# A recorded order of issue that counts the port VectorE and GpSimd share, and prices dense matmuls at 2.25 columns a ns

## Chip, cores and metric

The kernel runs on one core of one Trainium2 chip. The metric is the device time of one launch in microseconds (us): 2947.76 us before, the median of three runs (2943.65 to 2950.33). Engines are named as the profile names them: PE is TensorE (PEld its weight loads), DVE is VectorE, ACT is ScalarE, POOL is GpSimd, and SP is the queue from which nearly all DMAs are issued.

## What is computed

One layer of a hybrid encoder, 2048 prompt frames and 32 sample frames wide, 1024 features, float32 in and out. Cut to what matters here:

```python
def layer(x, ...):
    hn = rmsnorm(x, norm1)
    proj = jnp.einsum('btd,de->bte', hn, w_in)             # 1024 -> 3072
    pa_x, pa_g = proj[..., :D_A], proj[..., D_A:2 * D_A]   # RG-LRU, 256 wide
    pb = proj[..., 2 * D_A:2 * D_A + D_B_IN]               # RWKV-7, 6 heads of 64
    pc = proj[..., 2 * D_A + D_B_IN:]                      # mLSTM, 6 heads of 64
    ...
    ya = rmsnorm(h, norm_a) * jax.nn.gelu(pa_g)
    yb, shift_new, S_new = rwkv7_mix(pb, ...)              # a state carried from frame to frame
    yc, conv_c_new, C_new, n_new, m_new = mlstm_mix(pc, ...)
    y_mix = jnp.concatenate([ya, yb, yc], axis=-1)
    x = x + jnp.einsum('bte,ed->btd', y_mix, w_out)
    hn2 = rmsnorm(x, norm2)
    gu = jnp.einsum('btd,df->btf', hn2, w_ffn_in)          # 1024 -> 2 * 2816
    x = x + jnp.einsum('btf,fd->btd', jax.nn.silu(gu[..., :D_FF]) * gu[..., D_FF:], w_ffn_out)
```

The layer's outputs are the normed x and the running states of the three mixers.

## The kernel before

**Dense work.** Features lie on the partitions, frames on the columns. The 2080 frames are four column blocks: three of 512 and one of 544, which is worked as two halves of 272. Every projection is done in three matmuls for one, because weights and activations are split into a leading part and an exact rest: with `wh`, `wl` the weight's parts and `ah`, `al` the activation's, `mm3` issues `wh*ah`, `wh*al` and `wl*ah` into one PSUM tile `pj`. So the stages are, in dense matmuls: `inproj` 24 tiles x 8 row tiles x 3 = 576 a block, 1152 for the last one with its two halves, 2880 in all; `phase2` (output projection, FFN) 64 x 3 + 44 x 8 x 3 + 8 x 22 x 3 = 1776 a block, and 3552 for the last. Together 11760. Weights come by DMA (`raw`); ACT writes their leading part (`wh`, `hh`), DVE or POOL the rest (`wl`, `hl`).

**Mixers.** Between them stand the mixers: 16 groups of 128 prompt frames (0 to 15) and one of the 32 sample frames (group 16), each an RWKV-7 part (tiles `rw`), an mLSTM part (`ml`) and an RG-LRU part. A group's RWKV part is one chain through all engines: low-rank gates, key norms, the products `m1<-Fr,BK`, a round trip through DRAM (`tb<-Hr`, `xs<-tb`), a triangular solve of 31 steps on DVE (`utmp<-Z,xs`, then `Z<-Z,utmp`), a second round trip (`zb<-Z`, `c<-zb`), DVE's transpose `ta<-c`, the state's products on PE, a head norm on DVE (`hmE` to `yx`), three transposes on PE (`rw<-cst,yx`), and the result `E` to DRAM (`ymix<-E`). Groups follow each other through the state `S` and share their tiles.

**Which stage needs which group.** `phase2(i)` reads `ymix` of four groups, `sq<-ymix` and the split `al<-sq,ah`; `phase2(3)` that of groups 12 to 16. Row tiles 0 and 1 of `ymix` are RG-LRU's, 2 to 4 RWKV's, 5 to 7 mLSTM's, and a PSUM tile takes them in this order.

**Order of issue.** Nothing is issued when the code is run: a `Recorder` notes each instruction with its operands (`Recorder.add`) and gives it a price from `cost`. `Recorder.order` then plays the program through: the engine that can start first takes its most urgent instruction that is ready, and the sequence in which they were taken is the order in which each engine's queue is filled. Engines then run their queues strictly in that order. On PE the mixers (level 1) stand before the projections (level 2), but in bursts: their prices add to a `debt`, and the projections pay it back,

```python
                elif o.prio == 2:
                    debt -= o.dur * RATE
```

with `RATE` 0.45. So a price that is too low or too high moves nothing by itself: it decides how many dense matmuls stand between two steps of a mixer. Before the change a dense matmul of n columns was priced n / 2.4 + 2.7 ns (216.0 for 512, 116.0 for 272), and DVE and POOL ran side by side in the plan without any hold on each other.

Of the kernel before, what the change touches and what calls it, by code (L numbers as in the profile page):

```python
# [27 lines left out]
# columns of the per-feature vectors, 128 features a column  # L28
# [13 lines left out]
# columns of the constants  # L42
# [11 lines left out]
# columns of the small weights  # L54
# [41 lines left out]
class Cfg:  # L96
    def __init__(self, seq, sb1, sb2):
        # sb1: list of (prompt tokens, column blocks); the 32 sample tokens follow the last prompt token
        # sb2: list of (first column, column blocks)
        self.seq = seq  # L100
        self.T = seq + 32
        self.sb1 = sb1
        self.sb2 = sb2
# [10 lines left out]
# PE's share for the mixers, relative to the projections, and how long they may hold it at a time (ns)  # L114
RATE = 0.45
BURST = 1200.0
# allowance for the mixers' operands (ns)
# [13 lines left out]
# transfers issued ahead of the one under way (ns)  # L131
WINDOW = 3000.0
# the projection's tile before which the next columns are normed
NEXT = 14
# urgency, on the other engines and on PE; the lowest goes first
# [8 lines left out]
class Op:  # L144
    __slots__ = ("eng", "fn", "args", "kw", "dur", "lat", "prio", "succ", "need", "ready", "start", "end", "idx", "rank")


class Recorder:
    """Stands in for the engines: notes each instruction with its operands, so that the order of issue
    can be chosen before the instructions are emitted (under tc.manual_schedule, which keeps it)."""  # L150
# [49 lines left out]
    def add(self, eng, fn, name, args, kw):  # L200
# [12 lines left out]
        o.dur, o.lat = cost(eng, name, out, ins, kw)  # L213
        deps = set()
# [29 lines left out]
    def order(self):  # L244
        """greedy: the engine that can start first takes its most urgent instruction that is ready"""
# [5 lines left out]
        debt, burst = 0.0, False  # L251
        for o in self.ops:
            o.rank = (o.prio, o.idx)
            if o.need == 0:
                heapq.heappush(future[o.eng], (0.0, o.rank, o))
        out = []
        left = len(self.ops)
        while left:
# [36 lines left out]
            if best == "pe":  # L295
# [3 lines left out]
                elif o.prio == 2:  # L299
# [3 lines left out]
                    burst = False  # L303
            o.start = when
# [43 lines left out]
def cost(eng, name, out, ins, kw):  # L348
    """nanoseconds on the engine, and until another engine sees the result"""
# [8 lines left out]
    if eng == "pe":  # L358
# [3 lines left out]
        if st.dtype == F32R:  # L362
            return max(n, 256) / 2.4 + 2.7, 196.0
# [25 lines left out]

class Tiles:  # L390
    """fixed tiles, taken in turn: name -> bufs tiles"""
# [30 lines left out]
def hybrid_kernel(ctx, tc, A, O, cfg):  # L422
# [48 lines left out]
    def rsqrt_(x, y, t, it=3):  # L471
        """y = 1/sqrt(x), Newton from the exponent halved"""
# [7 lines left out]
    def log1p_(e, out2, tmp):  # L480
        """out2 = log(1+e)/2 for 0 <= e <= 1, by the series of atanh(e/(2+e)); tmp: two tiles"""
# [10 lines left out]
    # the gates' weights, row selections; histories and running states: stream 0 the prompt, 1 the sample  # L492
# [11 lines left out]
    def setup():  # L504
# [9 lines left out]
        # derived vectors  # L514
# [8 lines left out]
        # -4 softplus(-lam)  # L523
# [8 lines left out]
        # powers of two of silu's halves and of the key's scale  # L532
# [4 lines left out]
        # the gates' weights for the queries and keys, from the heads' input: wq wif_q + wk wif_k  # L537
# [18 lines left out]
        # wq wk^T: queries for keys that are the heads' input itself  # L556
# [5 lines left out]
        # selection rows for row terms in two parts  # L562
# [4 lines left out]
        # histories and running states  # L567
# [23 lines left out]
    def load_w(src, kt, eng=None, many=False, into=None):  # L591
        """a block of weights, split: (hi, lo) of each row tile. Two small ones share a slot;
        many: the hidden units' tiles serve as two slots more; into: tiles that are free"""
# [1044 lines left out]
```

## Time and profile before

| | before |
|---|---|
| three runs | 2943.65, 2947.76, 2950.33 us |
| profiled execution, span from first to last instruction | 2943.6 us, as the fastest of the three runs |
| PE busy | 2797.9 us (95%), granted clock 0.979 of full speed |
| DVE busy | 2190.3 us (74%) |
| ACT busy | 1217.7 us (41%) |
| POOL busy | 704.9 us (24%) |
| DMA | 317.95 MB, mean 108 GB/s |

A busy PE is not a PE at its peak: its matmuls are pipelined, and an instruction's duration (some 360 ns for a dense one) is longer than the time to the next. What a dense matmul takes is therefore read from long unbroken rows of them, and what PE loses from its idle time.

### The profile page before, as it was taken

The numbers are of one execution on the slowest core, as the hardware profiler recorded it, in microseconds if no ns is written. First come the engines' busy times: TensorE is split into PE (matmuls) and PEld (weight loads), VectorE is DVE, ScalarE is ACT, GpSimd is POOL, SyncE is SP. The second block draws the span as 40 slices with busy tenths as digits, with TensorE's granted clock in tenths as the row PEclk, the third lists the DMA queues.
The fourth block names the chain that finished last, engine by engine and source line by source line (L and its number), as shares of the span: only waits on it lengthen the run. The fifth ranks groups of instructions, "written<-read, shape, count | busy, mean of one in ns | idle before, by whom it ended". The sixth has DMA issues, their size and how long they took to land.

```text
span 2943.6 us, 48657 instructions
## 1 busy us (share of the span) xinstructions
PE 2797.9 (95%) x17643; PEld 2301.3 (78%) x17643; DVE 2190.3 (74%) x5580; ACT 1217.7 (41%) x2555; POOL 704.9 (24%) x839
## 2 busy tenths in 40 slices
PE   7989889989999999999999999999999999999998
PEld 6767667778877777777777777777777778999998
DVE  6776887777778877888888887888666776555555
ACT  4444454444454434445544444363433334322223
POOL 5644344344312011112311011122011112211102
PEclk9999999999999999999999999999999999999999
DMA  6353334253433233324433323334332334232222
GB/s 210 112 160 109 123 123 128 100 165 100 122 100 98 82 104 99 91 72 128 139 111 92 96 87 101 93 107 138 93 107 82 93 87 162 74 90 87 87 90 81
DMA packets 235212, 317.95 MB, mean 108 GB/s; under 512 B 63100, under 2 KB 146988, under 8 KB 234844
## 3 DMA queue, kind: packets, MB, share of 16 engines
q1 hardware_dynamic: 233820, 313.74, 35.0%
q8 instruction: 138, 2.26, 0.3%
q10 hardware_dynamic: 1152, 1.11, 0.1%
q14 instruction: 102, 0.84, 0.1%
HBM read 268.51 MB, written 46.27 MB: 107 GB/s over the span
## 4 chain that ended last, share of the span: by engine, by line
PE 61%; DVE 20%; DMA 5%; issue 2%; ACT 2%; POOL 1%; SPq 0%; DVEq 0%; ACTq 0%; POOLq 0%
PE pj L332 51%; PE rw L332 7%; DVE wl L332 4%; PE ml L332 3%; DMA xs<-tb 3%; DVE utmp L332 1%; DVE Z L332 1%; DVE stg L332 1%; DVE x L332 1%; DVE k L332 1%; DMA tb<-Hr 1%; DVE Fr L332 1%; DVE R L332 1%; DVE al L332 1%; DVE Dm L332 1%
## 5 line engine op out<-in xcount | busy, mean ns | idle before, releaser
L332 PE MATMUL pj<-ah,wh 128*128 128x512 f32 (+1 forms) x2560 | 905.8, 361 | 4.1 <-ACT cbuf L332 1.8
L332 PE MATMUL pj<-al,wh 128*128 128x512 f32 (+1 forms) x2560 | 903.8, 360 | 4.4 <-DVE al L332 4.4
L332 PE MATMUL pj<-ah,wl 128*128 128x512 f32 (+1 forms) x2560 | 836.4, 358 | 2.0 <-DVE wl L332 2.0
L332 ACT ACTIVATE wh<-raw 128x1024 fp32r<-128x1024 f32 (+2 forms) x444 | 382.2, 862 | 759.2 <-PE pj L332 587.5
L332 PEld LDWEIGHTS pj<-ah,wh 128*128 128x128 f32 x2560 | 488.6, 191 | 73.1 <-issue 2.7
L332 PEld LDWEIGHTS pj<-al,wh 128*128 128x128 f32 x2560 | 490.7, 192 | 69.2 <-DVE al L332 6.0
L332 PEld LDWEIGHTS pj<-ah,wl 128*128 128x128 f32 x2560 | 458.8, 191 | 71.4 <-DVE wl L332 3.0
L332 DVE TENSOR_TENSOR wl<-raw,wh 128x1024 fp32r<-128x1024 f32 (+2 forms) x397 | 412.6, 1041 | 61.7 <-ACT wh L332 58.7
L332 POOL TENSOR_TENSOR stg<-stg,rb 128x512 f32<-128x512 f32 (+1 forms) x110 | 155.2, 1419 | 893.8 <-DVE stg L332 771.0
L332 PE MATMUL pj<-hl,wh 128*128 128x512 f32 (+1 forms) x856 | 302.2, 360 | 2.7 <-DVE hl L332 2.1
L332 PE MATMUL pj<-hh,wh 128*128 128x512 f32 (+1 forms) x856 | 299.7, 361 | 3.5 <-ACT hh L332 3.5
L332 PE MATMUL pj<-hh,wl 128*128 128x512 f32 (+1 forms) x856 | 279.5, 356 | 0.0
L332 DVE TENSOR_TENSOR x<-x,pj 128x512 f32<-128x512 f32 (+1 forms) x280 | 159.1, 583 | 134.9 <-PE pj L332 133.2
L332 PEld LDWEIGHTS pj<-hl,wh 128*128 128x128 f32 x856 | 161.6, 189 | 28.3 <-DVE hl L332 7.0
L332 PEld LDWEIGHTS pj<-hh,wh 128*128 128x128 f32 x856 | 160.1, 188 | 28.8 <-ACT hh L332 6.7
L332 PE MATMUL pj<-ah,hh 128*128 128x512 f32 (+1 forms) x480 | 173.1, 367 | 7.3 <-ACT hh L332 5.8
L332 PE MATMUL pj<-al,hh 128*128 128x512 f32 (+1 forms) x480 | 174.7, 370 | 2.5 <-DVE al L332 2.5
L332 DVE TENSOR_TENSOR utmp<-Z,xs 96x60 f32<-96x60 f32 (+27 forms) x527 | 135.7, 258 | 51.1 <-DMA xs<-tb 36.4
L332 PEld LDWEIGHTS pj<-hh,wl 128*128 128x128 f32 x856 | 152.3, 188 | 22.3
L332 POOL TENSOR_TENSOR wl<-raw,wh 128x1024 fp32r<-128x1024 f32 x47 | 114.8, 2444 | 191.1 <-ACT wh L332 186.9
L332 PE MATMUL pj<-ah,hl 128*128 128x512 f32 (+1 forms) x480 | 160.1, 365 | 0.0
L332 POOL TENSOR_TENSOR hl<-raw,hh 128x512 fp32r<-128x512 f32 x92 | 126.7, 1379 | 114.6 <-ACT hh L332 106.1
(348 smaller groups left out, 4222.1 us busy)
## 6 DMA issues: line engine op xcount, KB each, us to landing
raw<-in_w_ffn_in SPq DMA_DIRECT2D x176, 512.0 KB
raw<-in_w_ffn_out SPq DMA_DIRECT2D x128, 256.0 KB
raw<-in_w_in SPq DMA_DIRECT2D x96, 256.0 KB
raw<-in_w_in SPq DMA_DIRECT2D x48, 512.0 KB
spill<-stg SPq DMA_DIRECT2D x72, 256.0 KB
raw<-in_w_out SPq DMA_DIRECT2D x32, 512.0 KB
x<-in_xT SPq DMA_DIRECT2D x48, 256.0 KB
raw<-in_w_ffn_out SPq DMA_DIRECT2D x64, 192.0 KB
```

Of the source, the lines that this page charges most:

```text
L332: o.fn(*o.args, **o.kw)
```

## The change

Two things are changed, and both only in the numbers by which the order is worked out. No instruction is added, removed or altered: each engine has the same work as before, in another order.

- A dense matmul of n columns is priced max(n, 256) / 2.25 + 4 ns: 231.6 for 512 columns, 124.9 for 272.
- An instruction is marked by `shares` when it is POOL's and has an input, or DVE's and has two inputs in SBUF that are wider than a column, or is a copy or a tensor-scalar with one such input. In the plan a marked one of DVE starts only when POOL's last marked one has ended, and the other way round.

The rest of the diff takes comments out.

```diff
@@ class Recorder, add
         o.dur, o.lat = cost(eng, name, out, ins, kw)
+        o.port = shares(eng, name, ins)
@@ order
         debt, burst = 0.0, False
+        port = {"dve": 0.0, "pool": 0.0}
...
                     burst = False
+            if o.port:
+                other = "pool" if best == "dve" else "dve"
+                when = max(when, port[other])
+                port[best] = when + o.dur
             o.start = when
@@ cost
         if st.dtype == F32R:
-            return max(n, 256) / 2.4 + 2.7, 196.0
+            return max(n, 256) / 2.25 + 4.0, 196.0
@@
+def shares(eng, name, ins):
+
+    wide = [a for a in ins if a.space != PSUM and not (len(a.ap) == 2 and int(a.ap[1][1]) == 1)]
+    if eng == "pool":
+        return bool(ins)
+    if eng == "dve":
+        return len(wide) > 1 or (len(wide) == 1 and len(ins) == 1 and name in ("tensor_copy", "tensor_scalar"))
+    return False
```

The two orders differ on every engine from the first rows on. Two places of PE's queue follow. The first is where group 3 ends, the last group that `phase2(0)` reads. In the order of before this is the row at which the last three transposes of group 3 stand (`rw_165<-cst_75,yx_169`), among dense matmuls of `inproj(3)` (`pj` from `ah`, `al` and the weight tiles `wh`, `wl`, 272 columns):

```order
L332 MATMUL pj_199<-ah_0_174,wh_143 128x272
L332 MATMUL pj_199<-al_0_175,wh_143 128x272
L332 MATMUL pj_200<-ah_0_174,wh_143 128x272
L332 MATMUL pj_200<-al_0_175,wh_143 128x272
L332 MATMUL pj_199<-ah_0_174,wl_145 128x272
L332 MATMUL pj_200<-ah_0_174,wl_145 128x272
L332 MATMUL rw_165<-cst_75,yx_169 128x128 x3
L332 MATMUL rw_166<-cl_123,bones_81 128x384
```

2274 dense matmuls stand ahead of these transposes, 606 fewer than `inproj` has. In the order of the change the same group is here only at the products that follow its solve (`rw_166<-ta_167,Hr_125`, the transposed block times `Hr`), and `inproj` is used up; the dense matmuls of 512 columns are the first of `phase2(0)`, from row tile 1:

```order
L338 MATMUL pj_198<-ah_0_172,wh_143 128x512
L338 MATMUL pj_198<-al_0_173,wh_143 128x512
L338 MATMUL pj_198<-ah_0_172,wl_145 128x512
L338 MATMUL ml_164<-cst_75,f_0_269 6x128
L338 MATMUL ml_164<-q_262,xi_261 64x64 x3
L338 MATMUL ml_163<-RS_84,selr_83 128x130 x3
L338 MATMUL rw_166<-ta_167,Hr_125 32x32 x12
L338 MATMUL ml_163<-cst_75,xi_261 128x128 x2
L338 MATMUL rw_165<-c_168,En_226 32x32 x12
L338 MATMUL rw_166<-SV_150,Fr_124 64x64 x6
L338 MATMUL ml_163<-cst_75,xi_261 128x128
L338 MATMUL rw_165<-zc_229,c_168 64x64 x6
```

What moved: 12 matmuls of `phase2(0)` stand ahead, those of row tiles 0 and 1; the next dense one, from `ah_0_174` (row tile 2, RWKV's), comes 46 rows after these 12 dense ones, and all rows between are mixers'. Group 3's last transposes stand behind 2892 dense matmuls.

The second place is group 16, the last that `phase2(3)` reads. In the order of before its chain has dense matmuls of `phase2(2)` (512 columns) between its steps; 212 of them stand between the first `rw` row here and the chain's row before it:

```order
L332 MATMUL pj_201<-ah_0_170,wh_142 128x512
L332 MATMUL pj_201<-al_0_171,wh_142 128x512
L332 MATMUL rw_165<-ta_167,Hr_125 32x32 x6
L332 MATMUL pj_201<-ah_0_170,wl_144 128x512
L332 MATMUL pj_201<-ah_0_172,wh_142 128x512
L332 MATMUL pj_201<-al_0_173,wh_142 128x512
L332 MATMUL pj_201<-ah_0_172,wl_144 128x512
L332 MATMUL rw_166<-c_168,En_226 32x32 x6
L332 MATMUL rw_165<-SV_150,Fr_124 64x64 x4
L332 MATMUL pj_201<-ah_0_174,wh_142 128x512
```

In the order of the change `phase2(2)` is used up. The dense rows are the last that `phase2(3)` has without RWKV's tiles (272 columns, row tile 1), and behind them stands the chain of group 16 from its key norms on: `zc`, the bonus `ch`, `cl`, the transposes `yx`, `m1` (`Fr_124,BK_240`), the block's transposes, the state:

```order
L338 MATMUL pj_200<-al_0_173,wh_143 128x272
L338 MATMUL pj_200<-ah_0_172,wl_145 128x272
L338 MATMUL rw_166<-cst_75,zc_229 64x96
L338 MATMUL rw_166<-ch_122,bones_81 128x192
L338 MATMUL rw_166<-cl_123,bones_81 128x192
L338 MATMUL rw_165<-cst_75,yx_169 128x64 x3
L338 MATMUL rw_165<-Fr_124,BK_240 128x128 x3
L338 MATMUL rw_166<-Fr_124,BK_240 128x128 x3
L338 MATMUL rw_165<-cst_75,BK_240 128x128 x3
L338 MATMUL rw_166<-cst_75,xs_223 64x128 x3
L338 MATMUL rw_165<-SV_150,Fr_124 64x64 x2
L338 MATMUL rw_165<-ta_167,Hr_125 32x32 x6
```

What moved: all of this chain, down to its last three transposes 13 rows further on, stands in PE's queue without a dense matmul between. Counted over the whole order, the dense matmuls ahead of a group's last transposes, beside the number at which the stage that reads it begins, are:

| last group read | stage begins after | before | change |
|---|---|---|---|
| 3, by `phase2(0)` | 2880 | 2274 | 2892 |
| 7, by `phase2(1)` | 4656 | 4261 | 4668 |
| 11, by `phase2(2)` | 6432 | 6063 | 6444 |
| 16, by `phase2(3)` | 8208 | 8166 | 8232 |

At groups 7 and 11 the rows between the last dense matmul and the first from row tile 2 begin later in the chain than at group 3: at 7 with the last products of the outputs (`rw<-SV,Fr`, `rw<-Un,Hr`), at 11 with the same products a few rows earlier, and 45 and 66 matmuls stand there, the mixers' but for eight at each.

## Rows read from the trace of the kernel before

**Rows 1.** The profile's page: span, busy time by engine, chain that ended last.

```profile
span 2943.6 us, 48657 instructions
PE 2797.9 (95%) x17643; PEld 2301.3 (78%) x17643; DVE 2190.3 (74%) x5580; ACT 1217.7 (41%) x2555; POOL 704.9 (24%) x839
...
PE 61%; DVE 20%; DMA 5%; issue 2%; ACT 2%; POOL 1%; SPq 0%; DVEq 0%; ACTq 0%; POOLq 0%
```

**Rows 2.** Busy time by stretch: start-up, input projection, phase2(0) to (2), phase2(3).

```profile
core 0: us, PE busy (x) PEld busy (x) DVE busy (x) ACT busy (x) POOL busy (x), PEclk, DMA share, GB/s
0.00:100.00 100.00, 84.68 (x365) 65.97 (x366) 59.43 (x97) 42.89 (x73) 56.93 (x73) 0.98 0.59 197
100.00:800.00 700.00, 631.61 (x4173) 515.13 (x4171) 539.95 (x1458) 321.89 (x736) 304.54 (x380) 0.96 0.39 123
800.00:2480.00 1680.00, 1636.12 (x9598) 1277.68 (x9598) 1348.79 (x3581) 713.31 (x1509) 265.96 (x317) 0.99 0.34 101
2480.00:2943.60 463.60, 445.51 (x3509) 442.51 (x3509) 242.15 (x447) 139.59 (x238) 77.44 (x69) 0.98 0.30 93
```

**Rows 3.** Chain that ended last, in order of time: start us, us, what.

```profile
2035.35 40.85 PE pj L332 x175
...
2578.72 69.85 PE pj L332 x554
```

**Rows 4.** PE's waits, 100 to 800 us: total us, times, longest.

```profile
PE rw L332 <- ACT ch L332: 9.9, 3, 6.1
PE ml L332 <- DVE gt L332: 8.1, 2, 5.4
PE ml L332 <- DVE QS L332: 6.2, 4, 2.8
PE ml L332 <- POOL WI L332: 4.4, 2, 2.3
```

**Rows 5.** POOL and DVE in order of time, 2286 to 2289 us: start us, us, instruction.

```profile
2286.37 2.28 POOL L332 TENSOR_TENSOR stg<-stg,rb 128x512 f32<-128x512 f32 x1 [15.37 <-DVE Z L332]
...
2286.29 1.22 DVE L332 TENSOR_TENSOR wl<-raw,wh 128x1024 fp32r<-128x1024 f32 x1
2287.42 1.31 DVE L332 TENSOR_TENSOR utmp<-Z,xs 96x63 f32<-96x63 f32 x1
2288.76 0.22 DVE L332 TENSOR_TENSOR Z<-Z,utmp 96x63 f32<-96x63 f32 x1
```

**Rows 6.** DVE in order of time: steps of group 15 behind its solve.

```profile
2314.97 0.38 DVE L332 STREAM_TRANSPOSE ta<-c 128x192 f32<-128x192 f32 x1 [0.39 <-DMA c<-zb]
...
2340.60 0.56 DVE L332 TENSOR_REDUCE hmE<-rw 128x6 f32<-128x384 f32 x1
...
2353.70 0.56 DVE L332 TENSOR_TENSOR E<-E,g 128x384 f32<-128x384 f32 x1
```

**Rows 7.** PE in order of time: key norms of group 16.

```profile
2356.36 0.31 PE L332 MATMUL rw<-sq,cst 128*32 128x64 f32 x6
```

**Rows 8.** DVE in order of time: group 16's solve, result, split.

```profile
2388.59 0.18 DVE L332 TENSOR_TENSOR utmp<-Z,xs 48x31 f32<-48x31 f32 x1 [0.91 <-DMA xs<-tb]
2388.81 0.18 DVE L332 TENSOR_TENSOR Z<-Z,utmp 48x31 f32<-48x31 f32 x1
...
2422.07 0.16 DVE L332 TENSOR_TENSOR Z<-Z,utmp 48x8 f32<-48x8 f32 x1
...
2459.78 0.36 DVE L332 TENSOR_TENSOR E<-E,g 128x192 f32<-128x192 f32 x1
...
2466.45 1.75 DVE L332 TENSOR_TENSOR al<-sq,ah 128x544 fp32r<-128x544 f32 x2 [0.60 <-ACT ah L332]
```

**Rows 9.** Busy time of the instructions on pj, in two stretches; columns as rows 2, without POOL.

```profile
2314.00:2356.00 42.00, 32.99 (x129) 22.80 (x127) 6.75 (x10) 0.00 (x0) 1.00 0.31 92
2356.00:2470.00 114.00, 105.19 (x439) 80.85 (x440) 23.15 (x35) 0.00 (x0) 0.99 0.32 97
```

**Rows 10.** Chain that ended last, 2350 to 2360 us.

```profile
2355.81 0.86 PE rw L332 x12
```

**Rows 11.** Busy time by stretch where phase2(3) begins; columns as rows 2.

```profile
2470.00:2486.00 16.00, 13.80 (x93) 13.26 (x92) 10.75 (x23) 5.02 (x7) 0.00 (x0) 0.87 0.65 226
2455.00:2470.00 15.00, 12.88 (x60) 10.56 (x59) 10.10 (x18) 11.60 (x20) 7.64 (x6) 0.91 0.64 220
```

More of the change, by code (lines that the diff above doesn't have):

```diff
@@ L144 @@
 class Op:
-    __slots__ = ("eng", "fn", "args", "kw", "dur", "lat", "prio", "succ", "need", "ready", "start", "end", "idx", "rank")
+    __slots__ = ("eng", "fn", "args", "kw", "dur", "lat", "prio", "succ", "need", "ready", "start", "end", "idx", "rank", "port")
 class Recorder:
```

## Prediction, made before the changed kernel had run

> **What bounds the kernel now.** I read the page first, then the stretches, then PE's waits. PE is busy 2797.9 of 2943.6 us and holds 61% of the chain that ended last [rows 1], so what can be won or lost is PE's idle time, 145.7 us. The stretches say where it lies [rows 2]: 15.3 us at the start, 68.4 us while the input projection runs (100 to 800 us), 43.9 us in the three middle stages (to 2480 us), 18.1 us in the last one. What PE waits for in the second stretch is almost all mixers' operands; the longest are `ch` from ACT, 9.9 us, and `gt` from DVE, 8.1 us [rows 4]. The last stretch is different in kind: there are no mixers in it, only dense matmuls end to end.
>
> **Part one, the dense price.** In unbroken rows 175 dense matmuls of 512 columns take 40.85 us, 233.4 ns each, and 554 of 272 columns 69.85 us, 126.1 ns [rows 3]. The old prices (216.0, 116.0) were 7 to 8% short of that, the new ones (231.6, 124.9) 1%. So far PE came to each mixer row later than planned, which gave the mixers' operands time. Between the last rows of groups 7 and 11 stand 6063 - 4261 = 1802 dense matmuls, 450 a group: at 17.4 ns each (233.4 less 216.0) that is 8 us a group of slack which the plan did not know of and which the new one spends. A second effect runs the other way: dense matmuls pay back the mixers' debt faster when they cost more, so 7% fewer stand between two bursts.
>
> The Trainium skill speaks against this part (TensorE: Matmul & The Clock Gate, Back-to-back issue gap): warm matmuls follow each other after N / 2.4 + 2.5 ns, 215.8 ns for 512, which is the old price. The trace does not agree with it here: 233.4 ns. By the page PE would come to the mixers' rows some 8 us a group earlier than planned now; the sum below goes by the trace.
>
> **Part two, the port.** That DVE and POOL hold each other up is in the trace: POOL's `stg` is on record from 2286.37 for 2.28 us while DVE's `wl` runs to 2287.51, and then DVE's `utmp` takes 1.31 us until POOL is done, where the same-sized next one takes 0.22 [rows 5]. POOL is busy 304.5 of 700 us while the input projection runs, DVE 540.0; together 844.5, more than the stretch [rows 2]. If they may not overlap, the plan must put the mixers later there, and the order shows that it does: group 3 ends 2892 dense matmuls into the queue, where it was 2274. It is a lag of one group, and it is never made up: groups 7, 11 and 16 too end after their stage's dense work is gone, by 12, 12 and 24 matmuls (those of row tiles 0 and 1, which need no RWKV). Before, 606, 395, 369 and 42 matmuls were still in hand. **In-order queues turn this into a wait that cannot be avoided:** at four places PE has nothing but the mixers' rows left until the group's result has gone to DRAM and come back.
>
> **What the four waits cost.** Each is the time of the rest of a chain, less PE's own work in it. The chains are on record only with dense work between their steps, which gives the upper bounds.
>
> At group 16 all from the key norms on is uncovered. In the trace that is from 2356.36 [rows 7] to the split at 2466.45 and 0.7 us of it [rows 8], 111 us. In this stretch PE gave 105.2 of 114 us to `pj` [rows 9], and this is what goes. The solve took 33.6 us (2388.59 to 2422.2); its first steps, unhindered, follow every 0.22 us, and 62 of them make 13.6 [rows 8]: 20 us less. Of the other 77 us I take three quarters, 58, since each step also waited behind dense rows on PE and behind splits on DVE; half would be 39. So 72 us, bounds 53 and 111. PE's own work in it is 60 matmuls; 12 of this kind take 0.86 us [rows 10], so 4 us. Lost: 68 us (49 to 107).
>
> At group 3 what follows the solve is uncovered: from `ta<-c` at 2314.97 to the end of `E<-E,g` at 2354.26, 39.3 us [rows 6], and from that row's end to the split's first tile 7.0 us (2460.14 to 2467.2) [rows 8]: 46 us as it ran, with 33.0 of 42 us of PE on `pj` [rows 9]. Three quarters are 35, half 23. The 142 mixers' matmuls there are 10 us of work. Lost: 25 us (13 to 36).
>
> At groups 7 and 11 the head norm and what follows is left: 2340.60 to 2354.26, 13.7 us [rows 6], and the same 7.0, so 21 us, three quarters 16, half 10, less 3 us of PE's work (45 and 66 matmuls, many of them tiny). Lost: 13 us each (7 to 18).
>
> Together 119 us (76 to 179). Off that goes what the last border cost so far, 2.2 us and 2.1 us of idle PE around 2455 to 2486 [rows 11], which a longer wait there swallows: 115 us. The clock adds a little: PE idle for 2.2 us of 16 brought the granted clock of that stretch to 0.87 [rows 11], which is 2 us at the lower of its levels, 1 us lost; four longer waits, and a chain of small matmuls at the lower level within the longest, I put at 4 us (0 to 10).
>
> **What the new order gives back.** While the input projection runs, mixers' steps are planned further apart and nearer to what DVE and POOL can do, so PE should meet fewer late operands. Of the 68.4 us I take 20 to be left, which is nearly the share that the middle stages have today (2.6%, 18 us of 700): 48 us back (0 to 68). In the middle stages POOL is busy 16% of the time [rows 2], so the port matters little there, while the slack of part one is gone. A group now has 444 matmuls beside it (6444 - 4668 over 4) where it had 450, 1.4 us less time for the same chain: if the chain set the pace, 12 groups would wait 17 us more; at best 30 us of the 43.9 go, if two thirds of them hang on mixers' rows. I take 6 us lost. Start and end hold the same steps; I put them at nothing, since no stage's work changes there (a reordered start-up could cost or give some 5 us of its 15.3).
>
> **Sum.** 2943.6 + 115 + 4 - 48 + 6 = 3020.6 us, to be compared with the span of 2943.6 us of the profiled execution, which lies 4.1 us under the median of the three runs. On the median's footing: 3025 us. The bounds together are 2943.6 + 72 - 68 - 30 = 2918 and 2943.6 + 175 + 10 + 17 = 3146; all ends at once are unlikely.
>
> **Rivals.**
> *The waits that go are worth more than the waits that come (faster).* One mechanism: DVE and POOL no longer run into each other because the order keeps them apart, so that PE's late operands vanish in all of 100 to 2480 us. At most 112 us (68.4 and 43.9) can come back so [rows 2]. It decides when the four waits cost less than comes back; at their lower bound (72 us) with 95 us back the time is 2921 us. For it: the waits in rows 4 hang on DVE and POOL. Against it: few of those waits are ended by POOL itself (4.4 us of these four rows), and the four new waits hang on chains, not on the port. The Trainium skill states the lock itself (SBUF — State Buffer, SBUF: two separate sides): the pair is held for a whole instruction, and the other engine "fully blocks". The trace agrees (1.31 us for 0.22), and by this rule alone a plan that knows the lock should win. Chance 0.06.
> *The slack mattered (slower still).* The middle stages lose 17 us, and group 16's chain runs hardly faster than with dense work between (107 us instead of 68): 3025 + 11 + 39 = 3075 us. For it: mixers' chains are bound by latencies that PE's dense rows never caused, such as the DRAM round trips. Against it: DVE was 75% busy in those stretches, and half its work there was dense. Chance 0.14.
> *Nothing that counts (same).* The mixers' rows at the borders run as fast as PE reaches them, as when a chain were ahead of its queue. Then only PE's own work stands there, and gains and losses in the rest cancel: 2948 us. The chain's earlier PE steps stand behind the last dense rows themselves, which excludes this at group 16 (49 us at least); only returns elsewhere could hide it. Chance 0.04.
>
> **How the numbers follow.** Forecast 0.76, at 3025 us; its own range, with the largest terms halfway to their bounds, is 2980 to 3070. The rival above takes 0.14 and the two below 0.10. For 8 in 10 I reach from 2975 to 3085: most of the slower rival lies inside, the two below outside. Three runs of this kernel spread over 0.2%, so a change within 0.2% could not be told from none. Faster 0.06, same 0.04, slower 0.90.
>
> **What would show each step.** Four gaps in PE's row at the borders of the stages, three of them near 0.8, 1.5 and 2.1 ms and of 10 to 30 us, one of 50 to 100 us near 2.45 ms with only `rw` matmuls in it; a lower clock there; the last stretch of dense matmuls as long as before (463.6 us) but for its beginning. PE's idle time inside the input projection should fall from 68 to some 20 us, that inside the middle stages stay near 44. POOL's and DVE's mean durations should fall a little if the order keeps them apart. I am wrong if the gaps are there but short (the chains run much faster alone than I allow), if the input projection gives back far more than 48 us, or if a fifth border appears, such as dense evacuation late on DVE.

## The result

The changed kernel is slower: 2993.49 us (median of four runs, 2989.22 to 2995.99) against 2946.62 us for the kernel before (four runs), a ratio of 1.0149 with a 95% interval of 1.0135 to 1.0163. That is 46.9 us more where 77 were forecast; the time lies inside the range of the prediction.

One correction first. The table of the change gives 2274, 4261 and 6063 as the dense matmuls ahead of the last transposes of groups 3, 7 and 11 before. These are one place too far: the rows quoted there (`rw<-cst,yx` followed by `cl`) belong to the next group's chain, behind its key norms. The right counts are 2187, 4197, 6011 and 8166, and PE's rows in the trace give the same; so before the change 693, 459, 421 and 42 matmuls were in hand, where the prediction has 606, 395, 369 and 42. The counts of the change stand. Dense matmuls in hand when a group that the next stage reads is done are called its lead below; of the changed kernel it is -12, -12, -12, -24.

The page of the changed kernel, its span, busy times and the chain that ended last:

```profile
span 2987.4 us, 48626 instructions
PE 2806.2 (94%) x17643; PEld 2309.9 (77%) x17643; DVE 2152.9 (72%) x5580; ACT 1226.0 (41%) x2555; POOL 718.5 (24%) x839
...
PE 76%; DVE 11%; DMA 7%; ACT 3%; issue 2%; POOL 1%; SPq 0%; DVEq 0%; ACTq 0%; POOLq 0%
```

Beside [rows 1] PE idles 181.2 us instead of 145.7 and is busy 8.3 us longer: 43.8 us together, the difference between the spans of the two profiled executions. Where the idle time lies is read from the stretches, cut here at four gaps between one dense matmul and the next (columns as [rows 2]):

```profile
0.00:100.00 100.00, 89.07 (x391) 70.43 (x392) 58.95 (x101) 48.54 (x84) 60.35 (x76) 0.98 0.61 202
100.00:712.60 612.60, 596.72 (x3827) 496.49 (x3826) 453.31 (x1181) 295.89 (x640) 298.30 (x365) 0.99 0.44 137
712.60:760.60 48.00, 28.75 (x268) 22.00 (x267) 34.08 (x118) 20.15 (x58) 3.68 (x11) 0.65 0.19 56
760.60:1316.10 555.50, 541.40 (x3209) 420.31 (x3209) 443.31 (x1211) 235.26 (x501) 91.87 (x106) 0.98 0.32 94
1316.10:1347.90 31.80, 12.95 (x79) 9.31 (x77) 24.25 (x91) 13.10 (x37) 3.27 (x5) 0.63 0.52 182
1347.90:1894.10 546.20, 536.45 (x3170) 414.35 (x3169) 449.32 (x1216) 237.58 (x503) 89.54 (x106) 0.99 0.33 96
1894.10:1928.20 34.10, 16.95 (x122) 12.05 (x120) 24.75 (x93) 13.23 (x37) 1.95 (x6) 0.66 0.48 164
1928.20:2461.10 532.90, 518.51 (x2923) 404.82 (x2923) 392.81 (x1008) 212.71 (x438) 88.16 (x91) 0.98 0.33 93
2461.10:2521.20 60.10, 14.77 (x108) 11.20 (x106) 29.12 (x118) 7.03 (x22) 2.49 (x7) 0.53 0.28 90
2521.20:2987.40 466.20, 450.67 (x3561) 448.96 (x3561) 242.97 (x449) 142.52 (x243) 78.88 (x69) 0.98 0.28 87
```

A row's first number behind the window is its length, the next PE's busy time: their difference is PE's idle time. The four gaps hold 19.3, 18.9, 17.2 and 45.3 us of it, 100.6 us, at a granted clock of 0.53 to 0.66. The input projection has 15.9 us left of 68.4, the start 10.9 of 15.3, the middle stages 14.1 + 9.8 + 14.4 = 38.2 of 43.9, the last stretch 15.5 of 18.1. So 100.6 us came and 65 went.

PE's waits now begin with the chain of a group (columns as [rows 4]):

```profile
PE rw L338 <- DVE ta L338: 24.4, 3, 23.6
PE rw L338 <- DVE yx L338: 22.0, 7, 10.0
PE rw L338 <- ACT ch L338: 17.8, 4, 5.1
```

The longest is the solve of group 16. PE in order of time through the last gap, from the key norms to the first dense matmul that reads RWKV's rows:

```profile
2458.18 0.44 PE L338 MATMUL rw<-sq,cst 128*32 128x64 f32 x6
...
2461.35 0.36 PE L338 MATMUL rw<-cst,zc 96*64 96x96 f32 x1
2465.34 0.53 PE L338 MATMUL rw<-ch,bones 128*128 128x192 f32 x1 [3.63 <-ACT ch L338]
...
2475.41 0.82 PE L338 MATMUL rw<-SV,Fr 128*64 128x64 f32 x4 [0.41 <-ACT SV L338]
2499.86 0.53 PE L338 MATMUL rw<-ta,Hr 32*32 32x32 f32 x12 [23.62 <-DVE ta L338]
...
2513.51 0.58 PE L338 MATMUL rw<-cst,yx 64*128 64x64 f32 x3 [5.27 <-DVE yx L338]
2521.23 1.27 PE L338 MATMUL pj<-ah,wh 128*128 128x272 f32 x4 [7.15 <-ACT ah L338]
```

And DVE's side of it, the first and last step of the solve and the transpose behind the second trip through DRAM:

```profile
2480.23 0.18 DVE L338 TENSOR_TENSOR utmp<-Z,xs 48x31 f32<-48x31 f32 x1 [6.13 <-DMA xs<-tb]
...
2494.74 0.16 DVE L338 TENSOR_TENSOR Z<-Z,utmp 48x8 f32<-48x8 f32 x1
2499.52 0.28 DVE L338 STREAM_TRANSPOSE ta<-c 128x96 f32<-128x96 f32 x1 [4.62 <-DMA c<-zb]
```

From key norms to the first dense row it is 63.1 us, where [rows 7, 8] had 110.8 with dense work between; the solve itself takes 14.7 us instead of 33.6.

### The profile page after: what moved, and what is told of

Read it like the earlier page. It is cut to its first block, busy times and chain, and to the rows that moved or that the text cites. A ratio compares the mean times of both kernels' runs of the same rounds, so it can differ in the third digit from the quotient of the medians.

```text
span 2987.4 us, 48626 instructions
## 1 busy us (share of the span) xinstructions
PE 2806.2 (94%) x17643; PEld 2309.9 (77%) x17643; DVE 2152.9 (72%) x5580; ACT 1226.0 (41%) x2555; POOL 718.5 (24%) x839
## 4 chain that ended last, share of the span: by engine, by line
PE 76%; DVE 11%; DMA 7%; ACT 3%; issue 2%; POOL 1%; SPq 0%; DVEq 0%; ACTq 0%; POOLq 0%
PE pj L338 63%; PE rw L338 9%; PE ml L338 4%; DMA xs<-tb 3%; DVE wl L338 2%; DVE Z L338 1%; DVE x L338 1%; DVE utmp L338 1%; DMA tb<-Hr 1%; DMA spill<-stg 1%; POOL stg L338 1%; DVE stg L338 1%; DMA xs<-spill 0%; ACT wh L338 0%; DMA c<-zb 0%
## 5 line engine op out<-in xcount | busy, mean ns | idle before, releaser
L338 DVE TENSOR_TENSOR wl<-raw,wh 128x1024 fp32r<-128x1024 f32 (+2 forms) x397 | 405.0, 1021 | 49.0 <-ACT wh L338 46.5
L338 POOL TENSOR_TENSOR stg<-stg,rb 128x512 f32<-128x512 f32 (+1 forms) x110 | 165.4, 1512 | 868.9 <-DVE stg L338 765.6
L338 DVE TENSOR_TENSOR utmp<-Z,xs 96x60 f32<-96x60 f32 (+27 forms) x527 | 126.4, 240 | 67.9 <-DMA xs<-tb 61.8
```

Source lines behind the costliest of these rows:

```text
L338: o.fn(*o.args, **o.kw)
```

## The experiments

My theory before them was that of the prediction, with the parts told apart: the port puts groups behind their borders and so makes the gaps; the price changes the mixture a little; an order that spares the gaps keeps what came back inside the stages and beats both kernels. The rivals were that the price itself costs, and that what came back cannot be had without the lag. In all of them the engines do the work of the changed kernel; only the order differs, in e8 also the order in which a PSUM tile takes its row tiles. All edits but that of e10 are made to the changed kernel.

**e1, the price alone.**

```diff
-        o.port = shares(eng, name, ins)
+        o.port = False
```

> Only the dense price is new; DVE and POOL run side by side in the plan as before. In the order the mixers end their last group with 946, 720, 768 and 564 dense matmuls still in hand at the four borders (before the change 693, 459, 421 and 42; with both parts none). Theory (the lag of one group, which the port makes, costs the time at four borders): no gap in PE's row at a border, PE's idle time in the input projection about as before (68 us), so 2930 to 2965 us. Rival (the price is what costs, because the slack of 8 us a group is gone): PE waits inside the stages grow, the time lies near 2990 us. Second rival (with the mixers further ahead, the last stage begins without any wait, and fewer dense matmuls stand between bursts): under 2930 us.

Measured: 3040.46 us, ratio 1.0313 (1.0292 to 1.0333). The theory missed; the price alone costs twice what both parts cost, which is the first rival's kind, 50 us past its number. No gap between dense matmuls is longer than 8.1 us, and the leads are large (946, 720, 768, 564): nothing waits at a border. The page, the stretch of the input projection, and PE's longest groups of waits:

```profile
PE 2843.6 (93%) x17643; PEld 2331.3 (77%) x17643; DVE 2188.6 (72%) x5580; ACT 1220.4 (40%) x2555; POOL 711.7 (23%) x839
```

```profile
100.00:700.00 600.00, 539.87 (x3255) 423.44 (x3254) 446.70 (x1195) 274.08 (x613) 252.21 (x295) 0.93 0.39 120
```

```profile
PE pj L338 <- ACT hh L338: 21.6, 9, 6.4
PE ml L338 <- POOL WI L338: 18.5, 7, 5.1
PE ml L338 <- DVE wl L338: 14.5, 8, 4.8
```

The span is 3046.9 us, in an execution 8 us above the median. Idle time is 203 us, 58 more than before, in many waits: added up by what PE was to do next, the rows of the mixers waited 151.8 us (105.8 before) and the rows on `pj` 41.8 (30.4), of which the longest group is the wait for `hh` above (21.6 us, 9.3 before). PE is busy 45.7 us longer. The granted clock of the stretch is 0.93 (before, from 100 to 700 us, 0.96), which goes with a part of that; how large a part, and what the rest is, was not taken apart.

**e2, the port alone.**

```diff
-            return max(n, 256) / 2.25 + 4.0, 196.0
+            return max(n, 256) / 2.4 + 2.7, 196.0
```

> Only the port is new; a dense matmul has its old price. In the order all four groups end after their stage's dense work is gone, as with both parts. Theory: four gaps at the borders, together 150 to 190 us from dense matmul to dense matmul (173.9 with both parts), the input projection's idle time under 30 us, so 2970 to 3005 us. Rival (the price is what costs): 2935 to 2950 us, no worse than before.

Measured: 3148.02 us, 1.0672 (1.0656 to 1.0688). Both ranges were missed. The kind of the theory was right, the size was not: four borders of 99 to 130 us, read here with the input projection ahead of them.

```profile
100.00:690.00 590.00, 576.09 (x3721) 482.61 (x3720) 417.26 (x1036) 284.40 (x609) 300.79 (x361) 1.00 0.44 137
692.00:791.10 99.10, 55.55 (x394) 43.86 (x392) 69.76 (x269) 33.76 (x96) 7.55 (x18) 0.58 0.21 61
1306.60:1418.80 112.20, 58.41 (x408) 44.25 (x406) 78.15 (x314) 33.80 (x99) 9.28 (x22) 0.54 0.27 83
1939.40:2051.50 112.10, 60.25 (x445) 46.87 (x443) 83.88 (x327) 35.41 (x105) 8.91 (x22) 0.57 0.27 79
2551.10:2680.80 129.70, 40.47 (x323) 33.08 (x322) 58.71 (x225) 19.42 (x62) 4.78 (x14) 0.53 0.18 53
```

Two things follow. The port's lag is much longer without the new price, at which dense matmuls pay the debt faster: the four stretches are 174 us with both parts and some 450 with the port alone. And the input projection idles 13.9 us of 590 with the old price too, so that what came back there is the port's.

**e3, half the hold.**

```diff
-                port[best] = when + o.dur
+                port[best] = when + 0.5 * o.dur
```

> Both parts, but a marked instruction holds the other engine only for half of its price. In the order 696, 405, 481 and 194 dense matmuls are in hand at the four borders. Theory (what costs is the lag at the borders, what gains is that late operands are planned for): no border gap, the input projection's idle time between that of before (68 us) and that of the change (16 us), so 2890 to 2935 us. Rival (the plan's holds themselves cost, since DVE and POOL are kept idle in turn): 2960 us or more. Rival (the give-back in the input projection was only the mixers' absence there, not better planning): no border gap, idle time there as before, 2935 to 2955 us.

Measured: 2970.59 us, 1.0072 (1.0051 to 1.0094). A miss. No border is uncovered (longest gap 7.5 us), but the input projection idles 49.2 us between 100 and 700 us, where no hold has 59.5 (before) and the whole one 15.8. Half a hold gives no half of the gain. The time is in the range of the first rival, that the holds themselves cost; but e7 below has the same hold and takes no longer than the kernel before, so that the hold is the cost isn't shown.

**e4, mixers ahead of the norms on DVE, ACT and POOL.**

```diff
-MIX = (1, 1)
+MIX = (-0.5, 1)
```

> Both parts in full, but on ACT, DVE, POOL and the DMA queue the mixers' instructions come ahead of the projections' ordinary ones (level 1 becomes -0.5 there; PE's levels stay). In the order 337, 269, 337 and 54 dense matmuls are in hand at the four borders, so the full hold is kept and the lag is gone. Theory: no border gap, 2890 to 2940 us. Rival (the hold costs, not the lag): 2970 us or more. A risk of its own: splits of weights and the normed input now wait behind mixers, and PE may wait for al, hl or hh; that would show as waits of dense matmuls, a few us in the change, 30 us or more here.

Measured: 2945.98 us, 0.9992 (0.9979 to 1.0005), the same as before, and between the ranges of theory and rival. The gaps are gone (longest 13.7 us) and the input projection idles 33.4 us, 26 less than before; but the middle stages give much of it back (columns as [rows 2]; the third row is the kernel before):

```profile
100.00:700.00 600.00, 566.56 (x3614) 462.07 (x3614) 454.55 (x1176) 288.81 (x629) 303.27 (x357) 0.96 0.43 131
700.00:2480.00 1780.00, 1706.62 (x10116) 1329.69 (x10115) 1415.13 (x3846) 749.72 (x1620) 287.32 (x346) 0.98 0.34 98
...
700.00:2480.00 1780.00, 1727.26 (x10358) 1362.05 (x10356) 1429.20 (x3827) 760.36 (x1631) 307.30 (x378) 0.98 0.34 102
```

73.4 us of the second row are idle, 52.7 in the third, and PE is busy 14.6 us longer in all. The profiled execution is 10 us above the median of its runs, so not all of these differences belong to the kernel.

The risk that the expectation names came: rows on `pj` wait longer. Over the whole execution their waits add up to 56.1 us (30.4 before, 33.9 with the change). In the input projection they are these four, 19.6 us, where the kernel before has the last line alone:

```profile
PE pj L338 <- DVE stg L338: 8.5, 3, 6.2
PE pj L338 <- POOL acc L338: 4.7, 1, 4.7
PE pj L338 <- ACT stg L338: 3.2, 2, 2.3
PE pj L338 <- DVE sq L338: 3.2, 1, 3.2
...
PE pj L332 <- DVE al L332: 0.8, 1, 0.8
```

The waits of mixers' rows in that stretch are 13.8 us, 58.5 before and 10.6 with the change. So the whole hold keeps the mixers' operands in time without the lag too; what is left there of the idle time is mostly that of rows on `pj`, whose operands now stand behind mixers on the other engines. Between 700 and 2480 us both kinds grew, rows on `pj` from 15.3 to 19.8 us and mixers' from 36.0 to 51.7.

Now the question was what the price alone loses. Theory A: PE meets the mixers' rows too early because the groups run far ahead. Rival B: what counts is the time the plan leaves between an operand and the matmul that reads it. `RATE` is the mixers' share of PE, `SLACK` an allowance. `Recorder.order` adds it ahead of every instruction of level 1 that depends on another, unless both are PE's; so it spaces the mixers' steps on DVE, ACT, POOL and the DMA queue as well, and not PE's operands alone, as the expectations have it. With `MIX = (-0.5, 1)` those engines' steps are no longer of level 1: e4 took the allowance from them together with the order of urgency.

**e5 and e6, the price alone at the leads of before, by two ways.**

```diff
-SLACK = 40.0
+SLACK = 90.0
```

> The new price alone, no port, with the allowance for a mixer's operand on PE raised from 40 to 90 ns; by the order the groups then stand 709, 458, 479 and 91 dense matmuls ahead of their borders, nearly where they stood before both changes (693, 459, 421, 42). Theory A (the time follows the lead: a group far ahead of its border means mixers' rows that come too early on PE, a group behind it means a gap): the 91 us that the price alone lost come back, 2940 to 2965 us, idle time of PE near 145. Rival B (the price itself costs, since the 8 us a group of unplanned slack are gone, wherever the groups stand): half of it stays, 2985 to 3020.

```diff
-RATE = 0.45
+RATE = 0.36
```

> The new price alone, no port, with the mixers' share on PE (RATE) cut from 0.45 to 0.36; the groups stand 754, 479, 451 and 93 ahead, again nearly where they stood before, but each operand has its old allowance of 40 ns. Theory A (lead decides): 2940 to 2965 us, as the run with the larger allowance. Rival B (the allowance in ns decides, bursts come to PE as close behind their operands as with the price alone): 3000 to 3045 us, with PE's waits near the 194 us of the price alone.

Measured: 2980.61 us (1.0115, 1.0099 to 1.0131) with the allowance, 3020.91 (1.0253, 1.023 to 1.0277) with the rate. The two have the same leads within 45 matmuls, and those of before within 61, yet the times are 2947, 2981 and 3021. Theory A falls. With the rate the time is in rival B's range; with the allowance it lies between the two ranges, 4 us under B's. 50 ns more of allowance win back 60 of the 91 us that e1 lost against its own kernel before (2949.17).

**e7, half the hold and 70 ns.** The edit is e3's with `SLACK = 70.0`.

> Both parts, the port held for half of an instruction's time, and the allowance raised from 40 to 70 ns; the groups stand 652, 384, 421 and 53 ahead, so no border is uncovered. Theory A (lead decides): the same time as before, 2935 to 2960 us. Rival C (a plan that knows port and price meets fewer late operands at the same lead): the input projection's idle time falls from 68 to under 40 us and the time to 2900 to 2930 us.

Measured: 2946.71 us, 0.9993 (0.9979 to 1.0006): the same as before, 24 us less than e3. The input projection idles 50.3 us between 100 and 700 us, so rival C, which asked for under 40, did not come. The time is in theory A's range, but e5 and e6 have refuted its reason. The allowance works elsewhere: from 700 to 2480 us PE idles 63.6 us (69.5 in e3), and it is busy 13 us less in all.

**e8, RWKV's row tiles last in the output projection.**

```diff
+LASTB = (0, 1, 5, 6, 7, 2, 3, 4)
-            for (o, N), ps in zip(bl, proj(w, act, bl)):
+            for (o, N), ps in zip(bl, proj([w[k] for k in LASTB], [act[k] for k in LASTB], bl)):
```

> The change as it is, but the output projection takes the row tiles of RWKV last (0, 1, 5, 6, 7, 2, 3, 4), so that more dense matmuls stand ahead of the wait at a border. Theory (a border's loss is the rest of the group's chain less what PE has to do in it): 18 more matmuls of 233 ns at three borders, 36 of 126 ns at the last, 4.2 to 4.5 us less idle time at each, 2972 to 2982 us instead of 2993. Rival (the mLSTM part of the group is as late as RWKV's, or the four PSUM tiles keep the further matmuls from standing ahead): the gaps stay, 2988 to 2998 us.

Measured: 3045.1 us, 1.0327 (1.0305 to 1.0349), 52 us slower than the change where 11 to 21 less were expected, and outside the rival's range too. The order again has 12 dense matmuls ahead and no more, and the gaps grew to 51.5, 59.1, 74.1 and 79.4 us. PE in the second of them:

```profile
1317.42 0.85 PE L339 MATMUL rw<-ta,Hr 32*32 32x32 f32 x24
...
1343.38 0.90 PE L339 MATMUL ml<-cst,wl 128*128 128x128 f32 x3 [3.11 <-DVE wl L339]
...
1367.39 1.22 PE L339 MATMUL pj<-ah,wh 128*128 128x512 f32 x2
```

Group 7's mLSTM part (`ml<-cst,wl` are its last transposes) is in the gap as well, so what the rival gave as its reason is there: mLSTM's part was as late as RWKV's. But the gaps did not stay. The dense rows run out at an earlier step of the chain: between the last one and the next stand 278 matmuls in the second gap and 318 in the third, both from the products behind the solve on (`rw<-ta,Hr` above), where the change has 77 and 119; and group 15's last transposes stand in the last gap too. Why this order leaves the groups further behind was not worked out.

**e9, allowance in place of the port.** The edit is e1's with `SLACK = 200.0`.

> The new price alone, no port, with the allowance for a mixer's operand on PE raised to 200 ns; the groups stand 352, 23, -12 and -24 ahead, so the last border is uncovered from the solve on and the third from the head norm on. Theory D (what the port did inside the stages was to plan mixers later behind their operands, which an allowance does too): 100 to 700 us have 20 to 35 us of idle PE (the price alone has 60, both parts have 16), the gaps at the last two borders are 20 to 75 us together, and the time 2930 to 2975 us. Rival E (only a plan that knows which instructions hold the port keeps PE's operands in time): idle in 100 to 700 us stays at 55 or more, and the time is 2985 to 3030.

Measured: 3055.95 us, 1.0361 (1.0342 to 1.0381). Idle between 100 and 700 us is 53.4, which is rival E's but for 2 us; the time is outside both ranges. No allowance tried without the port brought that stretch under 53 us. The gaps were far longer than I expected, 55.9 and 103.9 us; PE in the last one shows why:

```profile
2497.70 0.85 PE L338 MATMUL rw<-ta,Hr 32*32 32x32 f32 x24 [17.91 <-DVE ta L338]
...
2562.11 0.53 PE L338 MATMUL rw<-ta,Hr 32*32 32x32 f32 x12 [22.84 <-DVE ta L338]
```

There are two solves in it, group 15's (24 small matmuls) and group 16's (12). I had counted the lead of the last group alone; when group 15 is not done either, two chains stand one behind the other.

**e10, the kernel before with no allowance.**

```diff
-SLACK = 40.0
+SLACK = 0.0
```

> The kernel before (old price, no port) with the allowance for a mixer's operand on PE cut from 40 ns to none; the groups stand 798, 514, 498 and 170 ahead. It takes slack away in another way than the price does. Theory D (the price alone lost its time through slack): slower, 2975 to 3030 us, no gap over 12 us between dense matmuls, idle in 100 to 700 us above 60. Rival (slack is not what matters, the price itself spoils the mixture of rows): 2940 to 2960 us.

Measured: 3002.46 us, 1.0178 (1.0141 to 1.0216), as theory D has it: no gap over 7.3 us, 62.2 us idle between 100 and 700. At the old price too, 40 ns less before each of the mixers' steps cost 55 us (kernel before 2947.67).

**e11, three quarters of the hold.** The edit is e3's with 0.75.

> Both parts, the port held for three quarters of an instruction's time; the groups stand 43, -12, 45 and -24 ahead, so that of the four gaps of the change only those of the second and the last border can stay. If time is a sum of late operands inside the stages (which a longer hold lowers: 203, 147 and 181 less 101 us of idle PE at no, half and full hold) and gaps at the borders: two gaps of 25 to 60 us together 50 to 90, inside the stages 80 to 115 us idle, 2940 to 2965 us. Rival (a border's gap comes wherever the lead is under 100 dense matmuls): four gaps, 2965 to 2990 us.

Measured: 2979.82 us, 1.01 (1.0078 to 1.0123). The two gaps came where they should (17.4 and 58.2 us, together 75.6; the first shorter than expected), and the others did not. The time is in the rival's range, though not for its reason, which asked for four gaps. It missed the theory's range from above, since inside the stages less was won than I drew between half and whole: the gaps hold 51.8 of 181.8 us of idle PE, which leaves 130 where 80 to 115 were expected, 44.6 of them here:

```profile
100.00:700.00 600.00, 555.45 (x3487) 453.45 (x3486) 450.13 (x1147) 279.69 (x605) 297.34 (x350) 0.97 0.42 130
```

**e12, the whole hold, mixers first, a higher rate, a larger allowance.**

```diff
-RATE = 0.45
+RATE = 0.55
-SLACK = 40.0
+SLACK = 100.0
-MIX = (1, 1)
+MIX = (-0.5, 1)
```

> Both parts in full, the mixers first on DVE, ACT and POOL as in the earlier run, RATE 0.55 and an allowance of 100 ns; the groups stand 408, 407, 475 and 305 dense matmuls ahead, so no border is uncovered. If the full hold is what cures the input projection and the allowance what cures the middle stages: idle in 100 to 700 us 15 to 35 us (33 with mixers first alone), no gap over 10 us between dense matmuls, 2900 to 2930 us, faster than both kernels. Rival (a higher RATE, a thicker mixture of rows, gives back what the allowance wins): 2940 to 2965 us.

Measured: 2948.86 us, 0.9995 (0.9983 to 1.0007), the rival's number. The input projection idles 33.1 us as expected, but the middle stages 72.5 (700 to 2480 us), as in e4. Three gaps of over 10 us are there, the longest, 19.4 us near 0.7 ms, with PE busy on mixers' rows for 13.4. Rows on `pj` wait 59.9 us in all, 27.3 of them in the middle stages (19.8 in e4). Whether the rate did its part, as the rival has it, was not tested by itself; the larger allowance reached PE's rows alone, since `MIX` takes it from the other engines.

The runs side by side (idle is PE's, from 100 to 700 us; DVE and POOL their busy time from the page; in e4 and e12 the allowance is PE's alone):

| kernel | hold | allowance, ns | leads | idle | DVE | POOL | us |
|---|---|---|---|---|---|---|---|
| before | none | 40 | 693, 459, 421, 42 | 59.5 | 2190.3 | 704.9 | 2947 |
| e10 | none | 0 | 798, 514, 498, 170 | 62.2 | 2194.6 | 705.4 | 3002 |
| e1, new price | none | 40 | 946, 720, 768, 564 | 60.1 | 2188.6 | 711.7 | 3040 |
| e6, new price, RATE 0.36 | none | 40 | 754, 479, 451, 93 | 69.5 | 2198.0 | 707.9 | 3021 |
| e5, new price | none | 90 | 709, 458, 479, 91 | 63.2 | 2198.4 | 709.3 | 2981 |
| e9, new price | none | 200 | 352, 23, -12, -24 | 53.4 | 2195.1 | 713.6 | 3056 |
| e3 | half | 40 | 696, 405, 481, 194 | 49.2 | 2199.0 | 726.1 | 2971 |
| e7 | half | 70 | 652, 384, 421, 53 | 50.3 | 2196.8 | 719.7 | 2947 |
| e11 | 0.75 | 40 | 43, -12, 45, -24 | 44.6 | 2176.0 | 734.8 | 2980 |
| change | whole | 40 | -12, -12, -12, -24 | 15.8 | 2152.9 | 718.5 | 2993 |
| e2, old price | whole | 40 | -12, -12, -12, -24 | 17.3 | 2162.1 | 722.6 | 3148 |
| e8, tiles last | whole | 40 | -12, -12, -12, -24 | 19.6 | 2149.5 | 713.1 | 3045 |
| e4, mixers first | whole | 40 | 337, 269, 337, 54 | 33.4 | 2164.5 | 721.9 | 2946 |
| e12, mixers first, RATE 0.55 | whole | 100 | 408, 407, 475, 305 | 33.1 | 2150.6 | 722.2 | 2949 |

## Why the prediction was right, and where its sizes were off

**The four waits** are where they were forecast, and their sum, 119 us, measured 100.6. Group 16 was put at 68 and idles 45.3: the chain alone took 63.1 us for the 72 forecast (the solve 14.7 for 13.6; the rest of the chain 48.4 us, or 63% of what it took with dense work between, where I had taken three quarters), its first 3 us lay under the last dense rows, and PE's own work took 14.8 us of the gap at a clock of 0.53, not 4. Group 3 idles 19.3 for 25, in a gap of 48 us. Groups 7 and 11 were put at 13 and idle 18.9 and 17.2, and the stretches are 32 and 34 us. PE's own work was put far too low everywhere: 60, 142, 45 and 66 matmuls were counted at groups 16, 3, 7 and 11 and priced at 20 us together, and 105, 265, 77 and 119 stand there and take 73.4. The gaps were too short in the forecast as well, 139 us together where they are 174. The two errors nearly cancel in the idle time, so that its sum came out close is in part luck. What was missed at groups 7 and 11 is that other work stands in the same queues. DVE, in order of time ahead of group 7's last transposes, first does eight rows of the final norm of `phase2(0)`:

```profile
1324.65 5.09 DVE L338 TENSOR_TENSOR x<-x,acc 128x512 f32<-128x512 f32 x8
...
1332.76 0.56 DVE L338 TENSOR_TENSOR yx<-yx,h61E 128x384 f32<-128x384 f32 x1
```

The split `ah` that the first dense row reads stands on ACT behind the next group's `ch`, for which ACT waited, and on PE the row stands behind the product of `ch` (PE's rows first, then ACT's):

```profile
1333.37 0.90 PE L338 MATMUL rw<-cst,yx 128*128 128x128 f32 x3 [9.99 <-DVE yx L338]
...
1347.40 0.69 PE L338 MATMUL rw<-ch,bones 128*128 128x384 f32 x1 [4.80 <-ACT ch L338]
1347.92 1.22 PE L338 MATMUL pj<-ah,wh 128*128 128x512 f32 x2
...
1346.82 0.52 ACT L338 ACTIVATE ch<-c 128x384 fp32r<-128x384 f32 x1 [2.85 <-DVE c L338]
1347.25 1.65 ACT L338 ACTIVATE ah<-sq 128x512 fp32r<-128x512 f32 x3
```

**The clock** was put at 4 us; PE's busy time rose by 8.3, within the bounds given (0 to 10). Whether all of it is the clock is not shown. The reading behind the term was low by half: a granted clock of 0.87 over 16 us, between 1.2 and 2.4 GHz, is some 4 us at the lower level and 2 us lost, not 2 and 1.

**What comes back** was 48 us in the input projection and measured 52.5. From 100 to 700 us, before (first row) and with the change (columns as [rows 2]):

```profile
100.00:700.00 600.00, 540.47 (x3415) 430.77 (x3414) 459.55 (x1212) 274.84 (x614) 263.20 (x319) 0.96 0.39 124
100.00:700.00 600.00, 584.17 (x3739) 485.00 (x3738) 444.21 (x1134) 289.21 (x621) 297.72 (x364) 0.99 0.44 136
```

The cause holds: with the whole hold this stretch has 16 to 33 us of idle PE in each kernel that has it (e2, e4, e8, e12 and the change), with none 53 to 70, whatever the price, allowance or lead (before, e1, e5, e6, e9, e10). The waits of mixers' rows alone are 11 to 14 us with the whole hold and 44 to 66 with none. The two rows leave a rival: the lag took mixers' work out of the stretch, 1217 matmuls beside 1485 before, and fewer rows wait less. It does not explain the fall, for e11 has 1236 there and idles 44.6 us, and e4 has 1411 and idles 33.4. DVE's busy time over the same instructions falls from 2189 to 2198 us to 2150 to 2165. I read that as time for which DVE's instructions were held up; it is spread over many groups of them, and POOL's busy time, for which the prediction expected a fall too, rose by 13.6 us. Of the fall from 59.5 to 15.8 us, half a hold (e3) buys a quarter, and nothing of DVE's. The Trainium skill says that the pair is held for the whole instruction (SBUF — State Buffer, SBUF: two separate sides); these runs agree in so far as a plan with the whole hold is the only one that brought the idle time under 40 us. The rival "the waits that go are worth more" rested on the same rule; it needed more to come back than the borders cost, and 65 us came back against 100.6.

**The middle stages** were put 6 us worse and are 5.7 better; start and end, put at nothing, gave 4.4 and 2.6 us. The reason given was that the slack of part one is gone. That slack seems to matter more than the prediction gave it: alone the new price costs 91 us (e1), and a loss of this kind comes from a smaller allowance at the old price (e10). With both parts it does not show, and since an allowance without the port wins 60 us of it back (e5), I read the port's longer chains as allowance for the mixers' rows; this reading was not tested by itself. The bound of this term was too low as well: by the right counts a group had 453 matmuls beside it before, not 450, and lost 2.2 us rather than 1.4, which turns the bound of 17 us into 27.

So the parts do not add: 91 and 199 us alone (e1, e2, each against the kernel before beside it), 47 together. The port makes a lag that the price shortens (e2), and, by the reading above, the price takes slack away that the port gives back. The prediction read both from one order, that of the whole change, and so had the sum without having the parts. The rival "the slack mattered" was right on the price alone and wrong on the change, because its middle stages did not lose.

Still open is why no order beats the kernel before. Three orders with quite different holds, allowances and leads (e4, e7, e12) end within 0.1% of it, none clear of noise. In e4 and e12 the input projection's gain is on record and so is the loss: the rows on `pj` wait about twice as long as before, 56.1 and 59.9 us for 30.4, so that putting mixers first trades one kind of wait for the other. In the middle stages mixers' rows too wait longer (51.7 and 43.3 us for 36.0); that part is spread over many small waits, and its cause was not found.

## What to carry to other kernels

When prices of a plan are corrected, look at what their error was doing: a dense price 7% too low acted here like a reserve for small operands; correcting it alone cost 3%, and an explicit allowance won back two thirds of that. A plan that models one more conflict makes chains longer, so read first how far each chain then ends from the point that needs it, for the group before the last one too; behind in-order queues a lag turns into one wait for each border, however well the rest fits. Two corrections to one order are to be judged together and each alone, since neither's time says anything of the other's.

## What the runs showed of the hardware

With the same idle time in a stretch the granted clock was not the same: from 100 to 700 us it was 0.96 with 59.5 us idle (before) and 0.93 with 60.1 (e1), and 0.99 with 15.8 (change). PE's small rows in the gaps ran at 0.53 to 0.66, near the lower of the two levels (1.2 of 2.4 GHz), and the stretches between the gaps average 0.98 or 0.99. I had allowed for the clock at the borders only. Inside a stage it differs too, by what rule these runs do not show: with 62.2 us idle it was 0.97 (e10), with 33.4 it was 0.96 (e4).
